# Four modulation channels as row products on TensorE in the mixer's front, in place of dot products on VectorE

## The chip, the cores and the metric

The kernel runs on one core of a Trainium2 chip. A core has TensorE (PE in the profile; its weight loads are PEld), VectorE (DVE), ScalarE (ACT), GpSimd (POOL), and SyncE (SP), whose queue issues the DMA transfers here. The metric is the device time of one launch in microseconds (us), lower is better.

## What is computed

One layer of a diffusion backbone on 1024 latent tokens and 256 context tokens of width 1024: a SwiGLU block, a mixer (gated linear attention beside a gated spatial MLP), a second SwiGLU block, a final norm. The layer is modulated by nine channels of 1024 numbers, computed from a condition vector:

```python
def adaln(cond, w, b):
    return (jax.nn.silu(cond) @ w + b).reshape(cond.shape[0], ADA_MODS, 1, D_MODEL)
...
x = x + 0.5 * m_x[:, 2] * swiglu(modulate(rmsnorm(x, g1), m_x[:, 0], m_x[:, 1]), ff1_in, ff1_out)
y_x = modulate(rmsnorm(x, g2), m_x[:, 3], m_x[:, 4])
...  # mixer on y_x and on the context's y_c
x = x + m_x[:, 5] * mix_x
x = x + 0.5 * m_x[:, 8] * swiglu(modulate(rmsnorm(x, g3), m_x[:, 6], m_x[:, 7]), ff2_in, ff2_out)
```

So channel 5 is first needed by the mixer's output projection, channels 6 and 7 by the norm in front of the second block, and channel 8 by that block's last sums. `w` is 1024 x 9216 in fp32, 4 MB per channel. Channels 0 to 4 are needed for the latent condition `c` and for the context's `c_ctx`, channels 5 to 8 for `c` alone.

## The kernel before

Everything lies with the model's width on the 128 partitions, in 8 tiles (`NK`), and tokens along the free dimension, in blocks of 512, 512 and 256 (`TBS`). Matmuls that need accuracy are split into a high and a low part and run as three products (`gemm`, L357 to L360). The two SwiGLU blocks (`ffn`) are written as a seven-product scheme over pairs of 512-token blocks (`winograd`, L492).

The program is written in an order that a planner then changes: at build time it simulates all engines and takes, for each engine, the ready instruction that was written earliest (code in `high_priority` goes ahead). The order on each engine's queue is fixed then, and on the chip each engine works its queue in that order. Tiles come from pools by tag, with a fixed number of buffers per tag (`BUFS`): `raw` (2) takes weights as they land from DRAM, `w` (6) their high and low parts, `ar` (2) takes small loads and the dot products' weights, `po`, `pg` and `pn` are banks of PSUM, the accumulators (3, 3 and 2).

Modulation is done in two ways. Channels 0 and 1 (`ada_first`, `ada_rows`, `ada_cols`) are row products on PE at the very start: the condition's tile, 128 x 2, is the stationary operand, a weight tile of 128 x 1024 streams past it in two halves (L206), and after eight tiles a row of 2 x 1024 lies in PSUM; ScalarE copies it out, and small matmuls against the identity turn it into columns (L216). Channels 2 to 8 (`ada_part`) are dot products on VectorE: the weights are stored transposed (`wb`), a tile of 128 x 512 lands in `ar` (L167), and one instruction (L169, output `junk`, not used) multiplies it with the condition, which lies as a row on all partitions (`cr`, `cond_row`), and sums along the free dimension. There are 16 such tiles to a channel; after the last, L175 adds the halves and L155 the bias. Channels 2 to 4 are done during the first block, channels 5 to 7 in the mixer (48 tiles, written after the attention's second half), and channel 8 during the second block (16 tiles, `ada_todo`).

The mixer (`mixer`) begins with `mixer_front`: eight tiles of q, k and v are projected (`qkv_gemm`, output `z`), convolved by VectorE (`conv`, L791) and, for v, transposed (`tr`, L841). Each takes its weights through `raw` (L132), ScalarE makes the high part (L142), GpSimd the low one (L143). Then come the attention's states, scores and outputs (`ds` L1055, `sc` L1110, `o`). The gating's projections (`fill`: `vs`, `ogu`) are written late, and the planner puts them into PE's gaps from the front on. Next are the spatial gating (`gmlp_mix`, `mx`) and the output projection (`wo_add`): 32 sums of 12 matmuls each (`wo`), and each is added to x on VectorE with channel 5 as the scale (L1372). After each half of the tokens, `done2` computes the norm and the operands of the second block (`right_ops`, L453, L444), with channels 6 and 7.

Of the kernel before, what the change touches and what calls it, by code (L numbers as in the profile page):

```python
# [11 lines left out]
AF = mybir.ActivationFunctionType  # L12
ALU = mybir.AluOpType
# [3 lines left out]
P = 128  # L17
NK = 8
# [8 lines left out]
class Layer:  # L27
# [150 lines left out]
    def cond_row(self, j, c, dst):  # L178

        nc = self.nc  # L180
        n = c.stop - c.start
        t = self.tile(self.sb, 512, "ar", "cv")[:, :n] if n <= 512 else dst
        nc.sync.dma_start(t, self.a["cvec"][j:j + 1, c].to_broadcast([P, n]))
        nc.scalar.activation(dst, t, AF.Silu)
# [35 lines left out]
    def ada_first(self):  # L220

        pr = [[self.po("row") for _ in range(2)], [self.pg("row") for _ in range(2)]]
        for i in range(NK):
            for ch in range(2):
                self.ada_rows(self.a["wa"][ch], pr[ch], i)
        for ch in (1, 0):
            self.ada_cols(ch, pr[ch])

    def norm_coef(self, chs, gcol, nj, s):
# [733 lines left out]
    def mixer_front(self, y):  # L963

        nc, a = self.nc, self.a
# [29 lines left out]
        for dt in range(2):  # L995
            self.qkv_conv(ko[dt], 2 + dt, [self.k[0, dt], self.k[1, dt]], self.k[2, dt])
        vc = self.m("vc")
        for h in range(4):
            ct = self.h("ct")
            t = self.qkv_tile(y, a["wi"][2 + h], 4 + h, None, ct[:, :256])  # L1000
            if h % 2 == 0:
                v = [self.d("v") for _ in range(2)]
# [317 lines left out]
    def mixer(self, y, done=None):  # L1320
        nc, a = self.nc, self.a
# [6 lines left out]
        q1 = [self.queries(1, dt) for dt in range(2)]  # L1328
        row = self.d("cr")
        self.cond_row(0, slice(0, 1024), row)  # L1330
        for ch in (5, 6, 7):
            for h in range(2):
                for dt in range(NK):
                    self.ada_part(ch, dt, h, [row[:, h * 512:h * 512 + 512]])
        self.fill(y)
# [41 lines left out]
    def run(self):  # L1377
        nc, a = self.nc, self.a
# [67 lines left out]
        def done2b(tb):  # L1446
# [3 lines left out]
            for k in range(NK):  # L1450
# [5 lines left out]
                else:  # L1456
# [5 lines left out]
        self.ffn(mov, None, a["ff2i"], a["ff2o"], gates2, load_x2, None, self.squares(accs),  # L1462
                 done2b, self.ada_todo((8,), 1, 1, 16))

# [16 lines left out]
def pack(i):  # L1481
# [11 lines left out]
    o = {}  # L1493
# [14 lines left out]
    wa = i["w_ada"][0]  # L1508
    o["wa"] = c(wa.reshape(NK, P, 9, 1024)[:, :, :2].transpose(2, 0, 1, 3))
    o["wb"] = c(wa[:, 2048:].T.reshape(7, 8, P, 1024))  # L1510
    for s in ("ff1", "ff2"):
# [32 lines left out]
```

## Time and profile before

| | us |
|---|---|
| median of 3 runs | 2159.13 (2155.48 to 2160.04) |
| the profiled execution's own time | 2155.53 |
| its span, first to last instruction | 2153.8 |
| PE busy | 2015.6 |
| VectorE busy | 1503.2 |
| ScalarE busy | 816.5 |
| GpSimd busy | 379.9 |

Times inside the trace count from the span's start. The first block lies from about 120 to 900 us, the mixer from 930 to 1450, the second block behind it. A matmul's busy time is modelled and matmuls overlap in the pipeline, so the distance from one start to the next tells what a matmul costs, and a busy share near 100% tells that PE has no gaps. In fp32 a matmul shows as two records.

### The profile page before, as it was taken

Reading aid. Unit: us, or ns where it says so; the run is one execution under the profiler, and the core shown is the slowest. Engines: PE = TensorE matmul, PEld = TensorE weight load, DVE = VectorE, ACT = ScalarE, POOL = GpSimd, SP = SyncE. Lnnn points to the kernel's source line nnn. Section 1 sums busy time; section 2 is a strip of 40 time slices with the busy share of each in tenths; the row PEclk is TensorE's granted clock in tenths of the full one; section 3 lists DMA queues with packets and bytes.
Section 4 is the critical chain, followed back from the end, with each engine's and each line's share of the span. In section 5 each row is a group of like instructions: output and inputs, shape, how many; then the busy total and the mean of one; then the engine's idle time right before and its main releaser. Section 6 shows DMA issues by size and latency. Waiting matters only on the chain.

```text
span 2153.8 us, 28445 instructions
## 1 busy us (share of the span) xinstructions
PE 2015.6 (94%) x10868; PEld 1669.6 (78%) x10868; DVE 1503.2 (70%) x2503; ACT 816.5 (38%) x1297; POOL 379.9 (18%) x215
## 2 busy tenths in 40 slices
PE   6799999999999999898999998787999999999997
PEld 1678888888887888787788877565888888868875
DVE  3976665656655779869888377778677786755585
ACT  3643333333333121256456345325343444442111
POOL 0000000000025555223210010300000000065740
PEclk9799999999999999999999899897999999999998
DMA  7033333333368786321111126550444343458742
GB/s 286 25 127 118 123 142 118 122 118 118 118 222 340 275 295 240 147 79 54 49 56 50 35 91 219 200 183 28 166 158 165 112 181 137 182 216 350 306 143 79
DMA packets 111273, 332.27 MB, mean 154 GB/s; under 512 B 12448, under 2 KB 15392, under 8 KB 111136
## 3 DMA queue, kind: packets, MB, share of 16 engines
q1 hardware_dynamic: 111136, 330.45, 41.8%
q8 instruction: 85, 1.39, 0.3%
q14 instruction: 52, 0.43, 0.1%
HBM read 231.31 MB, written 99.09 MB: 153 GB/s over the span
## 4 chain that ended last, share of the span: by engine, by line
PE 72%; DVE 18%; DMA 5%; issue 2%; ACT 2%; POOL 0%; SPq 0%; DVEq 0%; ACTq 0%
PE c L492 14%; PE a L492 14%; PE f L492 14%; PE b L492 7%; DVE acc L791 3%; DMA ar<-in_wb 2%; PE gc L541 2%; PE gc L540 2%; PE gc L539 2%; PE row L206 1%; DVE hl L444 1%; PE o L541 1%; PE o L539 1%; PE o L540 1%; DVE junk L169 1%
## 5 line engine op out<-in xcount | busy, mean ns | idle before, releaser
L384 POOL TENSOR_TENSOR s<-raw 128x512 f32<-128x512 f32 x18 | 23.8, 1322 | 1149.0 <-DVE ch L526 602.0
L169 DVE SCALAR_TENSOR_TENSOR junk<-ar,cr 128x512 bf16<-128x512 f32 x160 | 112.5, 703 | 58.6 <-DMA ar<-in_wb 44.1
L390 ACT ACTIVATE gh<-raw 128x1024 fp32r<-128x1024 f32 x62 | 65.7, 1059 | 171.6 <-PE c L492 64.1
L492 PE MATMUL f<-hl,uh 128*128 128x512 f32 x528 | 126.8, 389 | 0.0
L443 ACT ACTIVATE hl<-g 128x512 fp32r<-128x512 f32 x106 | 64.3, 626 | 157.4 <-DVE g L526 153.0
L492 PE MATMUL a<-hl,gh 128*128 128x512 f32 x352 | 114.4, 403 | 8.8 <-ACT hl L443 6.3
L492 PE MATMUL c<-hl,sh 128*128 128x512 f32 x352 | 111.1, 393 | 11.7 <-ACT hl L443 9.6
L394 ACT ACTIVATE sh<-s 128x1024 fp32r<-128x1024 f32 x62 | 65.5, 1057 | 147.1 <-PE a L492 87.1
L492 PEld LDWEIGHTS f<-hl,uh 128*128 128x128 f32 x528 | 99.1, 188 | 20.6
L492 PE MATMUL b<-hl,gh 128*128 128x512 f32 x352 | 112.3, 396 | 0.8 <-ACT hl L443 0.8
L492 PE MATMUL a<-hl,sh 128*128 128x512 f32 x352 | 110.1, 393 | 1.0 <-ACT g L567 1.0
L492 PE MATMUL f<-hl,th 128*128 128x512 f32 x352 | 110.2, 390 | 0.8 <-ACT hl L443 0.8
L492 PE MATMUL c<-hl,th 128*128 128x512 f32 x352 | 108.9, 391 | 0.0
L526 DVE TENSOR_TENSOR u<-c,u 128x512 f32<-128x512 f32 x44 | 30.2, 687 | 109.0 <-ACT u L577 109.0
L791 DVE SCALAR_TENSOR_TENSOR acc<-z,par,acc 128x945 f32<-128x945 f32 (+2 forms) x64 | 93.1, 1477 | 11.6 <-ACT acc L813 10.5
L143 POOL TENSOR_TENSOR wl<-raw,wh 128x1024 fp32r<-128x1024 f32 x20 | 52.0, 2606 | 257.5 <-ACT wh L142 257.2
L444 DVE TENSOR_TENSOR hl<-g,hl 128x512 fp32r<-128x512 f32 x106 | 74.9, 724 | 26.1 <-ACT hl L443 26.0
L492 PEld LDWEIGHTS c<-hl,sh 128*128 128x128 f32 x352 | 66.4, 189 | 27.4 <-ACT hl L443 10.2
L385 DVE TENSOR_TENSOR sl<-s,sh 128x1024 fp32r<-128x1024 f32 x44 | 54.8, 1246 | 45.2 <-PE gc L540 21.9
L492 PEld LDWEIGHTS a<-hl,gh 128*128 128x128 f32 x352 | 67.1, 195 | 23.0 <-ACT hl L443 6.8
L492 PEld LDWEIGHTS b<-hl,gh 128*128 128x128 f32 x352 | 67.3, 191 | 15.8 <-ACT hl L443 1.8
L492 PEld LDWEIGHTS a<-hl,sh 128*128 128x128 f32 x352 | 66.6, 189 | 15.7 <-ACT g L567 1.3
(342 smaller groups left out, 6030.6 us busy)
## 6 DMA issues: line engine op xcount, KB each, us to landing
hd<-hl SPq DMA_DIRECT2D x142, 512.0 KB, 3.6
hc<-hd SPq DMA_DIRECT2D x142, 512.0 KB, 7.4
ar<-in_wb SPq DMA_DIRECT2D x112, 256.0 KB, 3.1
raw<-in_ff1i SPq DMA_DIRECT2D x44, 512.0 KB, 3.7
raw<-in_ff2i SPq DMA_DIRECT2D x44, 512.0 KB, 4.5
raw<-in_ff1o SPq DMA_DIRECT2D x22, 512.0 KB, 4.9
raw<-in_ff2o SPq DMA_DIRECT2D x22, 512.0 KB, 4.8
x<-in_xT SPq DMA_DIRECT2D x16, 512.0 KB, 6.8
```

The lines of the kernel that those rows point to most:

```text
L143: eng.tensor_tensor(out=lo[:, :n], in0=src[:, :n], in1=hi[:, :n].bitcast(F32), op=ALU.subtract)
L169: i = nc.vector.scalar_tensor_tensor(out=self.junk, in0=w, scalar=1.0, in1=cbc[j], op0=ALU.mult, op1=ALU.mult, accum_out=acc[:, h, dt, j:j ...
L385: sub = lambda o, x, y: eng.tensor_tensor(out=o, in0=x, in1=y, op=ALU.subtract)
L390: nc.scalar.activation(gh, g, AF.Copy)
L394: nc.scalar.activation(sh, s, AF.Copy)
L443: nc.scalar.activation(t[:, :512], src, AF.Copy)
L444: nc.vector.tensor_tensor(out=t[:, 512:], in0=src, in1=t[:, :512].bitcast(F32), op=ALU.subtract)
L492: mm = lambda x, y, start, stop: nc.tensor.matmul(ps, x, y, start=start, stop=stop, skip_group_check=more)
L539: nc.tensor.matmul(ps, hi[:, c], mh, start=i == 0, stop=False)
L540: nc.tensor.matmul(ps, hi[:, c], ml, start=False, stop=False)
L541: nc.tensor.matmul(ps, lo[:, c], mh, start=False, stop=i == n - 1)
L791: self.nc.vector.scalar_tensor_tensor(out=o, in0=zv[:, r0 + dr:r1 + dr, c0 + dc:c1 + dc], scalar=self.par[:, tap:tap + 1], in1=o, op0=ALU. ...
```

## The change

`ada_steps` is new: a generator that computes channels as row products on PE. For each pair of weight tiles it loads both through `raw` and issues four matmuls, each into its own group of 32 columns of PE's array (`g` = 0, 32, 64, 96: two weight tiles by two halves of 512). After eight tiles the four partial rows, two partitions each, are copied by ScalarE into a tile that was zeroed by VectorE, and a matmul with a selecting matrix `sel` adds the two groups of a half and turns them into columns. In `mixer_front`, channels 5, 6, 7 and 8 are made so, four steps behind each of v's four projections, one channel to a projection. The dot products of channels 5 to 7 in `mixer` and of channel 8 in the second block go, with their rows of the condition. The weights of these channels are stored as rows (`wa`) and no longer transposed (`wb`).

```diff
--- before.py
+++ after.py
@@ -179,7 +179,7 @@
 
         nc = self.nc
         n = c.stop - c.start
-        t = self.tile(self.sb, 512, "ar", "cv")[:, :n] if n <= 512 else dst
+        t = self.tile(self.sb, 512, "ar", "cv")[:, :n]
         nc.sync.dma_start(t, self.a["cvec"][j:j + 1, c].to_broadcast([P, n]))
         nc.scalar.activation(dst, t, AF.Silu)
 
@@ -225,6 +225,34 @@
                 self.ada_rows(self.a["wa"][ch], pr[ch], i)
         for ch in (1, 0):
             self.ada_cols(ch, pr[ch])
+
+    def ada_steps(self, chs):
+
+        nc = self.nc
+        sel = self.const([P, 2, 2], "sel")
+        for h in range(2):
+            nc.vector.tensor_tensor(out=sel[:, h], in0=self.ident[:, 32 * h:32 * h + 2],
+                                    in1=self.ident[:, 64 + 32 * h:66 + 32 * h], op=ALU.add)
+        for i, ch in chs:
+            pr = self.pn("row")
+            for k in range(0, NK, 2):
+                wts = [self.load(self.a["wa"][i, k + e]) for e in range(2)]
+                for e in range(2):
+                    for h in range(2):
+                        g = 64 * e + 32 * h
+                        nc.tensor.matmul(pr[g:g + 2], self.sc[:, k + e, :], wts[e][:, h * 512:h * 512 + 512],
+                                         start=(k == 0), stop=(k == NK - 2))
+                if k == NK - 2:
+                    row = self.h("row")
+                    nc.vector.memset(row, 0.0)
+                    for g in range(0, P, 32):
+                        nc.scalar.activation(row[g:g + 2], pr[g:g + 2], AF.Copy)
+                    pt = self.po("cols")
+                    for dt in range(NK):
+                        nc.tensor.matmul(pt[:, 2 * dt:2 * dt + 2], row[:, dt % 4 * P:dt % 4 * P + P], sel[:, dt // 4],
+                                         start=True, stop=True)
+                    self.ada_bias(ch, 2, pt[:, :2 * NK].rearrange("p (k j) -> p k j", j=2))
+                yield
 
     def norm_coef(self, chs, gcol, nj, s):
         A = self.const([P, NK, 2], "A" + s)
@@ -995,9 +1023,12 @@
         for dt in range(2):
             self.qkv_conv(ko[dt], 2 + dt, [self.k[0, dt], self.k[1, dt]], self.k[2, dt])
         vc = self.m("vc")
+        ada = self.ada_steps([(2, 5), (3, 6), (4, 7), (5, 8)])
         for h in range(4):
             ct = self.h("ct")
             t = self.qkv_tile(y, a["wi"][2 + h], 4 + h, None, ct[:, :256])
+            for _ in range(4):
+                next(ada)
             if h % 2 == 0:
                 v = [self.d("v") for _ in range(2)]
             for tb in range(2):
@@ -1326,12 +1357,6 @@
         on = [self.gla_norm(0, g0, [self.queries(0, dt) for dt in range(2)])]
         g1 = self.gla(1)
         q1 = [self.queries(1, dt) for dt in range(2)]
-        row = self.d("cr")
-        self.cond_row(0, slice(0, 1024), row)
-        for ch in (5, 6, 7):
-            for h in range(2):
-                for dt in range(NK):
-                    self.ada_part(ch, dt, h, [row[:, h * 512:h * 512 + 512]])
         self.fill(y)
         gm = self.gmlp_norm()
         with self.tc.high_priority():
@@ -1460,7 +1485,7 @@
 
         accs = {}
         self.ffn(mov, None, a["ff2i"], a["ff2o"], gates2, load_x2, None, self.squares(accs),
-                 done2b, self.ada_todo((8,), 1, 1, 16))
+                 done2b)
 
 
 def out_units(w):
@@ -1506,8 +1531,8 @@
         m[:, l] = ((np.arange(P)[:, None] % 64) >> l) ^ (np.arange(64)[None, :] >> l) == 1
     o["masks"] = m.reshape(P, 6 * 64)
     wa = i["w_ada"][0]
-    o["wa"] = c(wa.reshape(NK, P, 9, 1024)[:, :, :2].transpose(2, 0, 1, 3))
-    o["wb"] = c(wa[:, 2048:].T.reshape(7, 8, P, 1024))
+    o["wa"] = c(wa.reshape(NK, P, 9, 1024)[:, :, [0, 1, 5, 6, 7, 8]].transpose(2, 0, 1, 3))
+    o["wb"] = c(wa[:, 2048:5120].T.reshape(3, 8, P, 1024))
     for s in ("ff1", "ff2"):
         o[s + "i"] = c(col_tiles(i[s + "_in"][0]).reshape(2, NF, P, 1024).transpose(1, 0, 2, 3))
         o[s + "o"] = out_units(i[s + "_out"][0])
```

## Rows read from the trace of the kernel before

**Rows 1.** The page's totals: busy us, share of the span, instructions.
```profile
PE 2015.6 (94%) x10868; PEld 1669.6 (78%) x10868; DVE 1503.2 (70%) x2503; ACT 816.5 (38%) x1297; POOL 379.9 (18%) x215
```
**Rows 2.** The page's chain that ended last, shares of the span by line.
```profile
PE c L492 14%; PE a L492 14%; PE f L492 14%; PE b L492 7%; DVE acc L791 3%; DMA ar<-in_wb 2%; PE gc L541 2%; PE gc L540 2%; PE gc L539 2%; PE row L206 1%; DVE hl L444 1%; PE o L541 1%; PE o L539 1%; PE o L540 1%; DVE junk L169 1%
```
**Rows 3.** Busy us (and instructions) per stretch; then PE clock, DMA share, GB/s.
```profile
core 0: us, PE busy (x) PEld busy (x) DVE busy (x) ACT busy (x) POOL busy (x), PEclk, DMA share, GB/s
...
990.00:1050.00 60.00, 51.69 (x266) 43.07 (x265) 48.50 (x57) 37.08 (x71) 13.54 (x5) 0.97 0.19 62
1050.00:1115.00 65.00, 64.44 (x406) 57.79 (x405) 60.87 (x63) 27.73 (x52) 11.40 (x4) 1.00 0.13 43
1115.00:1180.00 65.00, 60.59 (x854) 54.39 (x853) 54.27 (x99) 41.81 (x76) 9.43 (x4) 0.97 0.18 60
...
1240.00:1320.00 80.00, 77.40 (x732) 62.42 (x730) 53.49 (x101) 46.70 (x77) 11.56 (x7) 0.94 0.40 139
1320.00:1344.00 24.00, 19.79 (x167) 15.41 (x166) 22.42 (x55) 5.62 (x9) 1.29 (x1) 1.00 0.57 195
1344.00:1356.00 12.00, 0.91 (x2) 0.81 (x3) 5.43 (x13) 5.41 (x6) 0.00 (x0) 0.59 0.96 375
1356.00:1450.00 94.00, 85.29 (x355) 65.86 (x354) 72.56 (x146) 22.80 (x36) 16.20 (x9) 0.98 0.53 173
1450.00:1503.00 53.00, 34.22 (x116) 24.86 (x116) 48.72 (x88) 33.69 (x56) 0.00 (x0) 0.77 0.12 41
```
**Rows 4.** PE's waits, 1320 to 1450: us in total, times, longest us.
```profile
PE wo L357 <- DVE x L1372: 19.5, 13, 11.6
```
**Rows 5.** VectorE's timeline: start us, us, instruction, idle time before it and its releaser.
```profile
1351.10 0.69 DVE L169 SCALAR_TENSOR_TENSOR junk<-ar,cr 128x512 bf16<-128x512 f32 x1 [5.15 <-DMA ar<-in_wb]
...
1353.61 0.17 DVE L155 TENSOR_TENSOR mods<-acc,par 128x8 f32<-128x8 f32 x1
...
1428.19 0.16 DVE L155 TENSOR_TENSOR mods<-acc,par 128x8 f32<-128x8 f32 x1
```
**Rows 6.** Groups by line, 1290 to 1450: busy us, mean ns, idle before, releasers.
```profile
L169 DVE SCALAR_TENSOR_TENSOR junk<-ar,cr 128x512 bf16<-128x512 f32 x48 | 36.4, 759 | 43.8 <-DMA ar<-in_wb 30.0 <-ACT cr L184 13.6
```
**Rows 7.** Tile wo, third of its three lines: min, median, max ns; first and last start.
```profile
L360 PE MATMUL wo<-ah,wo x128: 388/389/628, 1325.1 to 1449.0; 128*128 128x512 f32 x128
```
**Rows 8.** The chain in order of time: start us, us, what, instructions merged.
```profile
16.34 25.84 PE row L206 x60
42.18 2.78 PE cols L216 x24
...
123.17 2.72 PE c L492 x12
...
1165.31 1.02 PE ds L1055 x16
...
1172.04 0.44 PE tr L841 x4
...
1193.30 2.77 PE ds L1055 x48
...
1340.64 9.12 DMA og<-ogu
```
**Rows 9.** Busy us in a stretch of the second block, columns as in rows 3.
```profile
1920.00:1940.00 20.00, 18.23 (x75) 13.21 (x74) 6.64 (x12) 6.86 (x11) 13.32 (x8) 1.00 1.01 408
```
**Rows 10.** PE's timeline in the attention's scores.
```profile
1125.94 1.10 PE L1110 MATMUL sc<-x 64*64 64x64 f32 x60
```
**Rows 11.** DMA issues, 930 to 1130: KB each, median us to landing.
```profile
raw<-in_wi SPq DMA_DIRECT2D x10, 512.0 KB, 3.5
```
**Rows 12.** Groups by line, 990 to 1112, columns as in rows 6.
```profile
L143 POOL TENSOR_TENSOR wl<-raw,wh 128x1024 fp32r<-128x1024 f32 x9 | 24.9, 2771 | 89.4 <-ACT wh L142 89.4
...
L142 ACT ACTIVATE wh<-raw 128x1024 fp32r<-128x1024 f32 x9 | 9.6, 1072 | 17.7 <-issue 7.2 <-PE z L359 6.3 <-PE ogu L359 4.2
```
**Rows 13.** SP's timeline: the issue behind the first buffer given out.
```profile
984.67 0.33 SPq L132 DMA_DIRECT2D raw<-in_wi  x1
```
**Rows 14.** Tile z, 985 to 1100: min, median, max ns; first and last start.
```profile
L360 PE MATMUL z<-y,wl x144: 277/389/632, 995.0 to 1094.2; 128*128 128x512 f32 x96, 128*128 128x256 f32 x48
```

## The prediction, made before the change was run

> **What bounds the kernel now.** I read the engine totals first [rows 1]: TensorE (PE) is busy 94% of the span and VectorE (DVE) 70%, so a microsecond of PE work is dear and a microsecond of DVE work is cheap unless a stage says otherwise. Next the chain of waits as a whole [rows 2]: matmul lines lead it, but 2% is the landing of `ar<-in_wb`, the transposed weights of the dot products that the change removes, and 1% their instruction (`junk`, L169). So the removed work stands on the path somewhere, with about 43 + 20 us. Then the mixer by stages [rows 3], where the reader is to see two different regimes. From 990 to 1320 us PE is full: 51.7 of 60, 64.4 of 65, 60.6 of 65 and, at the end, 77.4 of 80 us. From 1344 to 1450 it is not: 0.9 of 12, then 85.3 of 94, and 34.2 of 53 us behind that. The change puts work into the first regime and takes work out of the second.
>
> Why PE stands still from 1343 to 1355 is in the waits and VectorE's timeline [rows 4, 5]: the output projection waits 19.5 us in all for the addition at L1372, once 11.6 us, because that addition multiplies by channel 5, whose last dot product (1351.10) had waited 5.15 us for its weights; the bias row (L155) follows at 1353.61, the additions behind it. For channels 6 and 7 it comes as late as 1428.19. In between VectorE works its queue in order, dot products and additions mixed. Over all it waits 30.0 us for weights, and 13.6 us before that for the row of the condition [rows 6]. PE has three accumulators for the projection, so each such wait soon reaches it.
>
> **The removed part, mixer.** The 48 dot products take 36.4 us of VectorE and 43.8 us of idle time before them [rows 6]. Not all of this is the kernel's: the time is what PE loses. The projection has 3 x 128 matmuls from 1325.1 to 1449.0 [rows 7]; at 12 in 2.72 us [rows 8] that is 87 of 124 us. Less some 7 us of other matmuls in between (the last of the gating, the spread of a norm), 30 us are lost, 11.6 of them for channel 5. The last reload, og, lands at 1349.8 [rows 8] and is needed only for the projection's second half, so PE would run on from about 1344; some 5 us of matmuls of the second block's first tiles also lie in that gap. I count 23 us gained to the end of the projection. After it, 1450 to 1503 is VectorE's (48.7 of 53 us busy [rows 3]): the norm and the operands of the second block for both halves of the sequence. The first half (8 modulations and 8 splits, 16 x 0.7 us, about 11 us) could run beside the second half of the projection, but waited for channels 6 and 7 and for the same queue. I count 8 of the 11. In 1320 to 1344 VectorE is busy 22.4 of 24 us with a dozen dot products (8 us) between the gating's additions; worth perhaps 1 us to PE. Sum 32 us; the bounds are 20 (the projection finds its next wait at the reloads of x and og) and 42 (30 + 11 + 1).
>
> **The removed part, second block.** 16 dot products of channel 8, 11 us of VectorE, and 4.2 MB of loads. PE is busy 18.2 of 20 us in 1920 to 1940, with the DMA engines full (1.01) [rows 9]. At 408 GB/s each 256 KB load is 0.64 us, 10 us for the sixteen if all fell in full stretches; PE shows 1.8 us lost in this one. I take 2 us (0 to 4).
>
> **The added part, PE.** Four channels x 8 weight tiles x 2 halves = 64 matmuls, 128 rows x 2 columns by 512, each two records. The nearest rows are the same matmuls at the start of the kernel, one after the other: 60 records in 25.84 us, 0.431 us each [rows 8]. In one column group the 128 records would be 55 us. The four groups may run side by side. Two groups of 64 columns do: 48 records `ds` in 2.77 us, 0.058 us each, where four full-width records `tr` of the same 128 elements take 0.44, 0.110 each, so 1.9 times as fast [rows 8]. Four tiles of 64 x 64 give 60 records in 1.10 us with ends included, 0.018 us each [rows 10], against half of 0.110 alone: three times. Four column groups at full height are not in the trace. Bounds: 55 / 4 = 14 us and 55 / 2 = 28 us (a pair of matmuls from one weight tile together, the other weight tile not there yet); below nothing cannot be, as all of it is new. I take 22. The Trainium skill, "TensorE: Matmul & The Clock Gate", section "Part 3: Packing small matmuls", says that matmuls start and end in strict order without reordering: as the two records of one matmul share a group, that rule would allow only pairs, 28 us in place of 22, and the whole sum would be -5, inside the range that I give the forecast. The trace speaks against it as a general limit, since in [rows 10] more than two records run at once.
>
> Entering and leaving the tiled shape costs about 0.1 us (16 `ds` records alone among others take 1.02 us, a third of 48 takes 0.92 [rows 8]); 16 to 32 times: 3 us. Turning the rows into columns: per channel 8 matmuls, 16 records, at 24 in 2.78 us [rows 8], 7.4 us for four. Sum on PE: 22 + 3 + 7.4 = 32 us (24 to 38). From 990 to 1050 PE idles 8.3 us and from 1115 to 1180 another 4 [rows 3], about 9 of which the new work can fill. All later PE work in the mixer (the projections kept in reserve for its gaps) is only pushed back, since PE is full to 1320. Net 23 us later.
>
> **The added part, everything else.** 16 copies on ScalarE of some 0.6 us (half of the 1024-wide copy's 1.07 [rows 12], rounded up), 10 us: hidden, ScalarE is busy 37 of 60 and 28 of 65 us there [rows 3]; uncovered they would hold 0.6 us of the cols matmuls each time. Four memsets and small sums on VectorE, 3 us: VectorE is busy 60.9 of 65 us there, but its queue waits for PE's tiles, so a later PE hides them. 32 loads of 512 KB by SP: the DMA share there is 0.13 to 0.19, 16.8 MB fit. But they go through `raw`, which has two buffers, ahead of the weights of the next projection tile in program order. One load holds its buffer for the landing (median 3.5 us [rows 11]), a pair of matmuls (0.9) and a wait for PE's order (about 0.9): 5.3 us, 2.65 per load with two buffers. A projection tile holds one for 3.5 us, ScalarE's 1.07 and GpSimd's 2.77 [rows 12]: 7.3, or 3.7. From 984.7 us, when a buffer is next given out [rows 13]: 32 x 2.65 + 5 x 3.7 = 103 us, so q's last weights come at about 1088, its matmuls (2 x 24 x 0.227 = 11 us per tile) end near 1108 instead of 1094.2 [rows 14]. That is 14 us, less than PE's 23: by this account the buffers don't set the end. Behind a waiting load on SP stand the stores of projected tiles, whose three buffers ScalarE needs; there are few in this stretch.
>
> **Sum.** +23 - 32 - 2 = -11 us against the profiled execution's 2155.53 us (span 2153.8): 2144.5. That execution lies 3.6 us under the median of the runs shown, 2159.13, so on that footing 2148.
>
> **Rivals.**
> 1. *Both buffers of `raw` become the bound: slower.* For it: SP already waits on them, matmuls and loads alternate on two buffers, and PE can do nothing else without weights that come through the same two. Against it: the account above leaves 9 us. It decides once a load holds its buffer for over 5.9 us ((23 - 14) / 32 x 2 more than 5.3), and makes the kernel slower from 6.6 us on (34 us late). At 7.5 us, one more wait of 2 us: 32 x 3.75 + 18 = 138 us from 985, q ends near 1143, 49 us late: +49 - 32 - 2 = +15, 2174.
> 2. *Full packing.* Groups run four at a time, the pairs arrive together, and the steps fall into gaps: PE 24, minus 10 of gaps, 14 net: 14 - 36 - 2 = -24, 2135. For it: [rows 10]. Against it: weight tiles land one by one.
> 3. *The gain goes elsewhere.* Projection and VectorE find the next wait (x and og reloads, then VectorE's 49 us for the second block): gain 20 only: +23 - 20 - 2 = +1, 2160. For it: og takes 9.1 us to land [rows 8], and VectorE is full from 1450 on. Against it: the dot products' own loads, 12.6 MB, leave that stretch.
> 4. *The steps don't pack at all:* 55 + 10 us, net 56: 56 - 34 = +22, 2181. The rows of two groups speak against it; I fold it into the first.
>
> **How the numbers follow.** Chances: forecast 0.47 (own range 2138 to 2158), rival 1 with 4 0.26, rival 2 0.17, rival 3 0.10. The best ends together, 14 - 42 - 4 = -32, give 2127, with 4 us below them for a plan made anew; above, rival 1's price is the end, and what is worse (49 - 20 = +29 and rival 4) is left out as about a tenth: 2123 to 2173. About 0.2%, 4.3 us, is what a measurement can tell from no change. Faster: 0.9 of the forecast's cases and rival 2, 0.59; slower: 0.26; the rest, most of rival 3, 0.15.
>
> **What would show it.** Right: no wait of L1372 near 1343, the projection's 384 matmuls in under 100 us, the second block's first full stretch some 10 us shorter behind it; the end of the q tiles' matmuls 15 to 30 us later than 1094; records of the new matmuls overlapping, two to four in 0.43 us. Wrong: PE idle in the front for loads of `in_wa`, new matmuls 0.43 us apart, or the projection still waiting as long. The schedule is planned anew for the whole mixer, so a different order of the reserve work could move either term by some 5 us.

## The result, and the profile after

The changed kernel took 2229.89 us (median of 4 runs, 2229.08 to 2231.8) against 2157.31 us (2152.95 to 2160.04) of the kernel before on the same chip: ratio 1.034 [1.0319, 1.036], 72.6 us slower. The forecast was 2148, the range 2123 to 2173.

The gain behind the front came as forecast. The front did not cost 23 us, but about 100.

Tiles z and wo of the changed kernel, third of their three lines, against [rows 14] and [rows 7]; lines L360, L357 and L1372 of before are L388, L385 and L1397 here:

```profile
L388 PE MATMUL z<-y,wl x144: 277/389/542, 1000.0 to 1193.5; 128*128 128x512 f32 x96, 128*128 128x256 f32 x48
...
L388 PE MATMUL wo<-ah,wo x128: 387/389/499, 1432.3 to 1527.4; 128*128 128x512 f32 x128
```

The last `z` matmul of the front starts at 1193.5 in place of 1094.2, 99.3 us later. The output projection starts 107.2 us later (1432.3 against 1325.1; of the 7.9 us more, 6.0 are one wait for ScalarE in the scan that grew from 0.7 to 6.7 us), takes 95.1 us in place of 123.9 (28.8 gained) and ends 78.4 us later. The span is 2230.0 against 2153.8, 76.2 longer, so another 2.2 us come back behind it, nearly all before the second block's first `c` matmul, which is at 1554.3 against 1478.2, 76.1 later. Sum: +107.2 - 28.8 - 2.2 = +76.2 us.

The wait of [rows 4] in the changed kernel (us in total, times, longest us):

```profile
PE wo L385 <- DVE x L1397: 1.2, 1, 1.2
```

19.5 us became 1.2. In the chain of waits by line, `junk` (L169) is no longer listed, and `ar<-in_wb` is now the weights of channels 2 to 4 in the first block alone; the loads of the rows' weights have come in (`DMA raw<-in_wa`), and the front's lines L385, L387 and L243, which [rows 2] does not have:

```profile
PE c L520 13%; PE f L520 13%; PE a L520 13%; PE b L520 7%; DMA ar<-in_wb 3%; DMA raw<-in_wa 2%; DVE acc L554 2%; PE gc L569 2%; PE gc L568 2%; PE gc L567 2%; PE row L206 1%; PE z L385 1%; DVE hl L472 1%; PE z L387 1%; PE row L243 1%
```

By stretches, to be read against [rows 3]:

```profile
core 0: us, PE busy (x) PEld busy (x) DVE busy (x) ACT busy (x) POOL busy (x), PEclk, DMA share, GB/s
990.00:1050.00 60.00, 49.46 (x233) 33.92 (x234) 42.17 (x59) 32.15 (x63) 5.57 (x2) 0.80 0.30 102
1050.00:1115.00 65.00, 48.78 (x218) 30.06 (x214) 21.51 (x23) 14.02 (x26) 2.35 (x1) 0.79 0.35 107
1115.00:1180.00 65.00, 49.90 (x204) 31.96 (x205) 13.16 (x15) 18.59 (x31) 9.41 (x4) 0.74 0.40 128
```

The regime in which PE was full is gone: 48.8 of 65 us where 64.4 were, and the granted clock, 0.97 to 1.00 before, is 0.74 to 0.80, a mixture of 1.2 and 2.4 GHz. No other engine is busy in its place, and the DMA share is 0.30 to 0.40. So nothing is at its limit; things wait for each other. PE's only waits from 1015 to 1170, and the longest wait of SP's queue from 1015 to 1180 (us in total, times, longest us):

```profile
PE row L243 <- DMA raw<-in_wa: 31.9, 15, 3.7
PE cols L252 <- ACT row L249: 9.9, 4, 2.5
...
SPq L132 <- PE row L243: 104.1, 28, 16.7
```

PE waits for the rows' weights and for ScalarE's copies of the rows, and SP waits for PE to be done with a buffer. How this comes about is in the timeline of one channel (start us, us, instruction, idle time before it and its releaser), first PE and ScalarE, then SP's issues:

```profile
1020.20 1.04 PE L243 MATMUL row<-raw,sc 128*2 128x512 f32 x8
...
1024.91 1.03 PE L243 MATMUL row<-raw,sc 128*2 128x512 f32 x4 [3.67 <-DMA raw<-in_wa]
...
1026.22 1.71 PE L243 MATMUL row<-raw,sc 128*2 128x512 f32 x4 [0.28 <-DMA raw<-in_wa]
...
1029.60 1.87 PE L243 MATMUL row<-raw,sc 128*2 128x512 f32 x4 [1.67 <-DMA raw<-in_wa]
...
1037.65 1.88 PE L243 MATMUL row<-raw,sc 128*2 128x512 f32 x4 [0.69 <-DMA raw<-in_wa]
...
1039.57 2.39 ACT L249 ACTIVATE row<-row 2x512 f32<-2x512 f32 x4 [4.04 <-PE row L243]
...
1041.98 1.06 ACT L142 ACTIVATE wh<-raw 128x1024 fp32r<-128x1024 f32 x1
...
1042.01 3.57 PE L252 MATMUL cols<-sel,row 128*128 128x2 f32 x16 [2.48 <-ACT row L249]
...
1045.44 1.95 PE L869 MATMUL tr<-ident,acc 128*128 128x128 f32 x8
...
1047.04 0.78 PE L385 MATMUL z<-y,wh 128*128 128x512 f32 x1
...
1063.90 1.04 PE L243 MATMUL row<-raw,sc 128*2 128x512 f32 x8
```

```profile
988.25 0.33 SPq L132 DMA_DIRECT2D raw<-in_wa  x1
...
1021.27 13.29 SPq L132 DMA_DIRECT2D raw<-in_wa  x6
...
1037.00 0.33 SPq L132 DMA_DIRECT2D raw<-in_wi  x1
...
1045.49 0.33 SPq L132 DMA_DIRECT2D raw<-in_wa  x1
...
1050.94 0.33 SPq L132 DMA_DIRECT2D raw<-in_wa  x1
...
1064.97 0.80 SPq L132 DMA_DIRECT2D raw<-in_wa  x2
```

The reader is to see three things that follow one another. The first load, issued at 988.25, waits in its buffer for PE's turn at 1020.20. From there to 1037.00 PE only takes row products as further loads land one by one (16.8 us; six in all, the sixth at 1037.65, with waits of 0.3 to 3.7 us). Then SP gets a buffer for the next projection tile (`in_wi`, 1037.00), and PE's first matmul with it is at 1047.04, 10.0 us later. In this time PE ends the channel: the last row step (1037.65), the wait for ScalarE's four copies (2.48 us), the columns to 1045.58, a few transposes. ScalarE splits the tile's high part behind its copies, by 1043.04, so here it is not the tile that PE waits for; by the list above PE never does. Then PE streams that tile to 1063.90 (16.9 us, a row step at 1049.45 among it), and meanwhile the two loads issued at 1045.49 and 1050.94 sit in both buffers, until SP issues again at 1064.97. That is 43.7 us for a value tile and a channel; the mean from channel to channel is 41.1 us (the sums of channels 5 and 8 come at 1045.6 and 1168.8).

### The profile page after: what moved, and what is told of

It reads as the page before. It is cut to its first block, busy times and chain, and to the rows that moved or that the text cites. A ratio compares the mean times of both kernels' runs of the same rounds, so it can differ in the third digit from the quotient of the medians.

```text
span 2230.0 us, 28613 instructions
## 1 busy us (share of the span) xinstructions
PE 2078.3 (93%) x11060; PEld 1697.3 (76%) x11060; DVE 1446.8 (65%) x2377; ACT 825.0 (37%) x1309; POOL 384.5 (17%) x215
## 4 chain that ended last, share of the span: by engine, by line
PE 74%; DVE 14%; DMA 7%; ACT 2%; issue 2%; SPq 0%; POOL 0%; DVEq 0%; ACTq 0%
PE c L520 13%; PE f L520 13%; PE a L520 13%; PE b L520 7%; DMA ar<-in_wb 3%; DMA raw<-in_wa 2%; DVE acc L554 2%; PE gc L569 2%; PE gc L568 2%; PE gc L567 2%; PE row L206 1%; PE z L385 1%; DVE hl L472 1%; PE z L387 1%; PE row L243 1%
## 5 line engine op out<-in xcount | busy, mean ns | idle before, releaser
L819 DVE SCALAR_TENSOR_TENSOR acc<-z,par,acc 128x945 f32<-128x945 f32 (+2 forms) x64 | 82.8, 1307 | 65.8 <-ACT acc L841 64.9
L418 ACT ACTIVATE gh<-raw 128x1024 fp32r<-128x1024 f32 x62 | 65.6, 1059 | 159.2 <-PE c L520 48.8
L554 DVE TENSOR_TENSOR u<-c,u 128x512 f32<-128x512 f32 x44 | 30.2, 686 | 109.6 <-ACT u L605 109.6
L520 PEld LDWEIGHTS c<-hl,sh 128*128 128x128 f32 x352 | 66.5, 189 | 27.3 <-ACT hl L471 10.2
L169 DVE SCALAR_TENSOR_TENSOR junk<-ar,cr 128x512 bf16<-128x512 f32 x96 | 65.3, 680 | 22.2 <-DMA ar<-in_wb 21.2
```

What stands on the lines that cost most here:

```text
L169: i = nc.vector.scalar_tensor_tensor(out=self.junk, in0=w, scalar=1.0, in1=cbc[j], op0=ALU.mult, op1=ALU.mult, accum_out=acc[:, h, dt, j:j ...
L418: nc.scalar.activation(gh, g, AF.Copy)
L520: mm = lambda x, y, start, stop: nc.tensor.matmul(ps, x, y, start=start, stop=stop, skip_group_check=more)
L554: tt = lambda eng, o, x, y, op: eng.tensor_tensor(out=o, in0=x, in1=y, op=op)
L819: self.nc.vector.scalar_tensor_tensor(out=o, in0=zv[:, r0 + dr:r1 + dr, c0 + dc:c1 + dc], scalar=self.par[:, tap:tap + 1], in1=o, op0=ALU. ...
```

## The experiments

Theory A: the two `raw` buffers and PE's order pass the new loads and the projections' weights one behind the other. Theory B: PE's own new work (its packing, its clock) is the cost. Theory C: ScalarE's row copies, which stand ahead of the next split. Each run's difference is to the kernel before on the same chip; "period" is the mean distance of the channels' sums.

| run | median us | difference us | ratio, 95% interval | last z us | period us |
|---|---|---|---|---|---|
| changed kernel | 2229.9 | +72.6 | 1.034 [1.0319, 1.036] | 1193.5 | 41.1 |
| x1_none | 2124.2 | -36.1 | 0.9833 [0.9801, 0.9865] | 1094.9 | - |
| x2_resident | 2145.2 | -15.1 | 0.9922 [0.9899, 0.9944] | 1115.8 | 19.0 |
| x3_loads | 2198.2 | +37.9 | 1.0176 [1.0143, 1.0209] | 1162.0 | 34.0 |
| x4_open | 2194.6 | +34.2 | 1.0159 [1.0127, 1.019] | 1165.0 | 34.1 |
| x5_ar | 2255.0 | +94.2 | 1.0436 [1.04, 1.0471] | 1153.9 | 57.6 |
| x6_ar_open | 2254.7 | +93.9 | 1.0434 [1.04, 1.0468] | 1148.0 | 58.1 |
| x7_fill | 2237.3 | +76.5 | 1.0353 [1.0327, 1.0378] | 1094.0 | 36.3 |
| y1_crh | 2156.6 | -4.2 | 0.9979 [0.9967, 0.9991] | 1093.3 | - |
| x8_w | 2155.5 | -1.0 | 0.9989 [0.9978, 1.0001] | 1126.0 | 27.3 |
| x8_w_open | 2159.9 | +3.3 | 1.0003 [0.9986, 1.002] | 1130.5 | 27.7 |
| z1 (5 to 7) | 2151.3 | -5.2 | 0.9977 [0.9961, 0.9993] | 1116.0 | 27.5 |
| z2 (5) | 2147.9 | -11.6 | 0.995 [0.9934, 0.9966] | 1100.7 | - |
| z3 (5, 6) | 2147.4 | -12.2 | 0.9949 [0.9929, 0.9968] | 1110.2 | 30.4 |

**x1_none: the gain alone.** The steps' loads and matmuls are gone; the bias alone is added.

```diff
-                wts = [self.load(self.a["wa"][i, k + e]) for e in range(2)]
...
-                    self.ada_bias(ch, 2, pt[:, :2 * NK].rearrange("p (k j) -> p k j", j=2))
+                    self.nc.vector.tensor_copy(
+                        self.mods[:, ch],
+                        self.par[:, C_BADA + 8 * ch:C_BADA + 8 * ch + 8].unsqueeze(2).to_broadcast([P, NK, 2]))
```

> The changed kernel without any row product: channels 5 to 8 hold their bias alone (their products with the condition are left out of the computation). The tail's gain stays, the front's cost goes. Theory A (the two `raw` buffers pass the new loads and the projections' weights one behind the other) and theory B (the new matmuls' own time on PE, slow clock and order) say the same: the last z and q matmul at 1094 to 1100 us as before (1193.5 in the changed kernel), the projection's 384 matmuls in some 97 us as in the changed kernel, total 2157 - 31 = 2126 us (2115 to 2135). If the total stays above 2150, the tail's gain was not there and both fall.

36.1 us faster by the medians, 30.2 by the profiled spans (2123.6 against 2153.8; the profiled execution of before, 2155.53, lies 5 us under 2160.33, the median of the kernel before on this run's chip). The front is that of before (last z 1094.9), the projection takes 95.6 us. So the gain is there in full, and the row products cost the changed kernel 108.7 us (+72.6 against -36.1), 98.6 of them by the last z matmul.

**x2_resident: PE's work without loads.**

```diff
+        res = self.h("res")
+        nc.sync.dma_start(res, self.a["wa"][2, 0, :, :512])
...
-                wts = [self.load(self.a["wa"][i, k + e]) for e in range(2)]
...
-                        nc.tensor.matmul(pr[g:g + 2], self.sc[:, k + e, :], wts[e][:, h * 512:h * 512 + 512],
+                        nc.tensor.matmul(pr[g:g + 2], self.sc[:, k + e, :], res,
```

> All 64 row matmuls stay, with their shape and place, but stream one 128x512 weight tile that is loaded once into another buffer; the 32 loads through `raw` are gone (the true weights of channels 5 to 8 are left out). Theory A (buffers): the front costs only PE's work, 24 to 38 us: last z matmul at about 1120 (1112 to 1130), total 2145 to 2165. Theory B (PE's own time): the last z matmul stays near 1180 to 1195, total 2215 to 2232. Theory C (ScalarE's four row copies per channel stand ahead of the next tile's split, 2.4 us times 4 channels): would leave at most 10 us above theory A's figure.

21.0 us above x1_none, and the last z 20.9 us later: all that PE's own work and the copies cost without loads. Theory B falls as the main cause, and C with it, since the copies on ScalarE are all still there; behind late rows they cost PE the 9.9 us of waits shown above. The timeline, the group of the row products (busy us, mean ns, idle before), and the first stretch:

```profile
1031.34 3.62 PE L244 MATMUL row<-res,sc 128*2 128x512 f32 x32
1040.86 1.84 PE L253 MATMUL cols<-sel,row 128*128 128x2 f32 x16
...
L244 PE MATMUL row<-res,sc 128*2 128x512 f32 x128 | 15.3, 592 | 0.0
...
990.00:1050.00 60.00, 55.40 (x332) 42.46 (x331) 48.49 (x59) 38.42 (x73) 12.70 (x5) 0.97 0.16 49
```

32 records in 3.62 us is 0.113 each, a fourth of the 0.431 of [rows 8]: where the weights are there, four column groups run side by side.

**x3_loads: the loads with little of PE's work.** Each row matmul streams 2 columns, and ScalarE copies 2 in place of 512.

```diff
-                        nc.tensor.matmul(pr[g:g + 2], self.sc[:, k + e, :], wts[e][:, h * 512:h * 512 + 512],
+                        nc.tensor.matmul(pr[g:g + 2, :2], self.sc[:, k + e, :], wts[e][:, h * 512:h * 512 + 2],
...
-                        nc.scalar.activation(row[g:g + 2], pr[g:g + 2], AF.Copy)
+                        nc.scalar.activation(row[g:g + 2, :2], pr[g:g + 2, :2], AF.Copy)
```

> All 32 loads of 512 KB through `raw` stay, in their place, but each row matmul streams 2 columns in place of 512 (the rest of channels 5 to 8 is left out). PE's new work is almost nothing. Theory A (buffers): a load still holds its buffer until its matmul, so only about 0.9 us of some 8.8 us per pair goes: the last z matmul at 1165 to 1190, total 2195 to 2228. Theory B (PE's own time): last z matmul near 1100 to 1110, total 2126 to 2140.

74.0 us above x1_none, as theory A has it; the total is inside what was expected, the last z, 1162.0, 3 us before it. Of PE's new work the columns' matmuls are left (14.3 us busy) and 5.6 us of rows. PE's waits for loads, 1015 to 1140 us:

```profile
PE row L243 <- DMA raw<-in_wa: 46.3, 21, 3.7
```

Loads 74, matmuls 21, both 108.7: at least 14 us, since the columns' matmuls are in both runs, are where the one makes the other longer.

**x4_open: the projection's weights first.** The same steps, but the next projection tile is loaded and split ahead of the channel's steps.

```diff
-            t = self.qkv_tile(y, a["wi"][2 + h], 4 + h, None, ct[:, :256])
+            for tb in range(3):
+                self.qkv_gemm(o, y, 4 + h, tb, ct[:, :256])
+            nxt = self.qkv_open(a["wi"][3 + h])
+            t = self.qkv_conv(o, 4 + h, None, ct[:, :256])
+            o = nxt
```

> The whole computation; the weights of the next projection tile are loaded and split before the channel's four steps in place of behind them, so that PE has a full projection tile to stream while the eight loads of a channel pass the two `raw` buffers. Theory A (order in the buffers): eight loads at 2.65 to 3.7 us each are 21 to 30 us, beside them 14 us of a projection tile plus 8 of new work: a period of 25 to 32 us in place of 41, the last z matmul 35 to 65 us earlier (1130 to 1160), total 2165 to 2195. If the order is all that costs, 2150. Theory B (PE's own time): no change, 2222 to 2232.

The total is at the upper edge of what theory A expected; the period of 34.1 us misses its 25 to 32, and the last z, 1165.0, its 1130 to 1160. The order in the buffers is worth 38 us (72.6 - 34.2), a third of the 108.7 us. Nine loads in 34.1 us are 3.8 us each, so a buffer is held 7.6 us, though the loads land as fast as before (in_wa, issues from 1015 to 1160: KB each, median us):

```profile
raw<-in_wa SPq DMA_DIRECT2D x30, 512.0 KB, 3.7
```

The other 3.9 us would then be the matmuls and the wait for their turn in PE's order, which now stands among the projection's matmuls; this is worked out, not seen.

**x5_ar and x6_ar_open: own buffers, half tiles.** The rows' weights come as 128x512 halves through the two buffers `ar`; x6_ar_open has x4_open's order as well.

```diff
-                wts = [self.load(self.a["wa"][i, k + e]) for e in range(2)]
...
+                        wt = self.tile(self.sb, 512, "ar", "wa")
+                        nc.sync.dma_start(wt, self.a["wa"][i, k + e, :, h * 512:h * 512 + 512])
```

> The whole computation; the row products' weights come as 128x512 halves (256 KB) through the two buffers `ar` and no longer through `raw`, which keeps only the projections' weights. Order and place unchanged. Theory A as the runs so far sharpen it (PE's part is 21 us, the rest of the front's cost is that loads and projection weights pass two buffers in turn): the projection tiles can be fetched while a channel's loads run, so the two chains lie beside each other: 16 halves by some 4 us through two buffers are 32 us per channel if a half lands as slowly as a whole tile, 24 if it lands in 3: a period of 24 to 33 us in place of 41, total 2165 to 2200. Theory A' (the shared buffers are the whole cost, a half lands fast): 2145 to 2155. Theory B (PE's own time and slow clock): 2225 to 2232.

> x5_ar and x4_open together: own buffers, and the next projection tile's weights opened before the channel's four steps. If what x4_open left (34 us per channel) was that the eight loads and the projection's load still share two buffers, own buffers give a shorter period here, 22 to 30 us, and a total of 2150 to 2185, below both x4_open and x5_ar. If it was the time that two buffers take to pass 4.2 MB at one load of 3.6 us each, whichever buffers they are, it stays within 10 us of the better of the two.

Both miss far, upwards; x6_ar_open also misses its 10 us around the better of the two, which was x4_open. For x5_ar a load of a half and the row products' group:

```profile
wa<-in_wa SPq DMA_DIRECT2D x64, 256.0 KB, 2.7
```

```profile
1175.24 1.02 PE L244 MATMUL row<-wa,sc 128*2 128x512 f32 x2
...
L244 PE MATMUL row<-wa,sc 128*2 128x512 f32 x128 | 65.0, 599 | 11.9 <-DMA wa<-in_wa 11.9
```

Half the bytes land in 2.7 us where the whole tile takes 3.6 to 3.7, so two buffers of halves bring less per us. The Trainium skill, "SBUF — State Buffer", section "The DMA setup-cost knee (why "@ 1 MiB" ≠ asymptote)", says that each transfer pays some 2 us whatever its size; the 2.7 us for half the bytes agree with that direction. And with one half there at a time one column group runs alone: the row products take 65.0 us of PE in place of 15.3. That is the case of rival 4, made by the landing and not by TensorE. It is not the whole of the 94 us. PE waits only 11.9 us for these loads. The scan comes behind the last row step: its first scores start at 1258.3 (1203.0 in the changed kernel). The reserve of projections is used up among the row steps (PE 100.0 of 100 us busy from 1155 to 1255), and from 1258 to the output projection the granted clock is 0.75, with 15.1 us of waits for VectorE (L1126; 0.2 at the same line of the changed kernel). So these two runs say little on the buffers alone.

**x7_fill: the same steps in the reserve of projections.**

```diff
+        ada = self.ada_steps([(2, 5), (3, 6), (4, 7), (5, 8)])
         for j in (6, 7, 0, 1, 2, 3):
...
                 self.project(w, y, j, tb, self.last_level if j == 3 and tb else None)
+                for _ in range(2):
+                    next(ada, None)
```

> The whole computation; the sixteen steps move from the front's value tiles to the reserve of projections (`fill`), two behind each projected half, where `raw` gives out a buffer only some ten times between 1100 and 1320 us in the kernel before. Theory A: the loads then land beside the scan's matmuls, only PE's 21 us stay, and the tail keeps its gain of 36: the last z matmul at 1094 to 1100, total 2140 to 2160, as with the resident weight tile (2145). If instead the scan's order leaves PE waiting for single loads there too, 2160 to 2190. Theory B: above 2200.

A miss: the front is free of it (last z 1094.0), but the same cost appears in the scan. The total lies where theory B was put, above 2200; it is x2_resident and x8_w that speak against B, not this run. From 1230 to 1390 us:

```profile
L243 PE MATMUL row<-raw,sc 128*2 128x512 f32 x128 | 43.2, 773 | 24.4 <-DMA raw<-in_wa 24.1
```

The steps were planned back to back, 1234.6 to 1373.0, and again two loads at a time feed them. The granted clock is 0.70 to 0.79 there. Buffers that stand idle on average don't help steps that come in a bunch.

**x8_w: six buffers.** Whole tiles again, loaded into `w`.

```diff
-                wts = [self.load(self.a["wa"][i, k + e]) for e in range(2)]
+                wts = [self.w("wa") for _ in range(2)]
+                for e in range(2):
+                    nc.sync.dma_start(wts[e], self.a["wa"][i, k + e])
```

> The whole computation; the 512 KB tiles of the row products are loaded into buffers of the tag `w` (six, of which a projection tile needs two) in place of `raw`, so that up to four of them can be under way at once and `raw` is left to the projections' weights. Whole tiles, so a pair of records in two column groups comes with each landing, as in the changed kernel. Theory A'' (what costs is the number of loads under way: a buffer's hold, landing plus the wait for PE's order, divided by the buffers): eight holds of 5 to 8 us over four buffers are 10 to 16 us per channel, beside them 14 us of projection and 5 of new work on PE: a period of 19 to 25 us, last z and row matmul near 1120 to 1140, total 2145 to 2170. If landing time is a matter of bytes and not of buffers (256 KB halves through `ar` came at 1.87 us each), the pace stays 3 us per tile and more: total 2195 to 2230. Theory B (PE's own time, slow clock): 2225.

> As x8_w, and the next projection tile's weights are opened (loaded and split) before the channel's four steps, so two of the six `w` buffers stand ready and fewer are left to the new loads. If the number of loads under way is what counts, no better than x8_w and up to 20 us worse; if the late projection weights still cost, 5 to 20 us better than x8_w.

This settles it between the buffers and PE's own work. The same loads, matmuls and copies, written at the same place, take 2155.5 us in place of 2229.9, by another tag for a buffer. The tag changes two things at once: there are six buffers, and the rows' weights no longer share `raw` with the projections' (in `w` they stand beside these tiles' high and low parts). Total and last z are within what was expected, the period of 27.3 us above its 19 to 25. The timeline of the first channel, the group of the row products, and the stretches:

```profile
1017.34 1.90 PE L245 MATMUL row<-wa,sc 128*2 128x512 f32 x16
1021.01 1.03 PE L245 MATMUL row<-wa,sc 128*2 128x512 f32 x4 [1.77 <-DMA wa<-in_wa]
1022.42 1.03 PE L245 MATMUL row<-wa,sc 128*2 128x512 f32 x4 [0.39 <-DMA wa<-in_wa]
...
L245 PE MATMUL row<-wa,sc 128*2 128x512 f32 x128 | 24.0, 592 | 7.3 <-DMA wa<-in_wa 7.3
```

```profile
990.00:1050.00 60.00, 54.81 (x315) 41.01 (x315) 47.73 (x62) 36.29 (x71) 8.32 (x3) 1.00 0.45 161
1050.00:1115.00 65.00, 62.34 (x326) 40.84 (x323) 34.38 (x31) 27.14 (x47) 11.59 (x5) 1.00 0.51 176
```

Four tiles stand ready for the first channel, 16 records run in 1.90 us, and the clock stays at 1.00. Row products take 24.0 us of PE and wait 7.3; in the changed kernel it was this group:

```profile
L243 PE MATMUL row<-raw,sc 128*2 128x512 f32 x128 | 41.7, 838 | 31.9 <-DMA raw<-in_wa 31.9
```

Opening the projections early on top of it (x8_w_open) brings nothing, as was expected if the number of loads under way counts.

**y1_crh: the gain without the move.** The kernel before, its dot products started earlier by another buffer for the condition's row.

```diff
-        row = self.d("cr")
-        self.cond_row(0, slice(0, 1024), row)
+        rows = [self.h("cr") for _ in range(2)]
+        for h in range(2):
+            self.cond_row(0, slice(h * 512, h * 512 + 512), rows[h])
```

> The kernel before, dot products on VectorE and all, but the condition's row stands in two 512-wide `h` buffers in place of a 1024-wide `d` buffer, which came free only at 1292 us: the dot products may start in VectorE's idle time between 1180 and 1240 us, and channel 5 is done before the projection needs it. If what the change gained behind the front (31 to 36 us) was the late start of the dot products, this gains much of it with nothing on PE: 2125 to 2145. If it was VectorE's share of work itself, 2150 to 2160. If the dot products delay the scan's own additions, slower than 2160.

4.2 us: the gain of an early start (2125 to 2145) is missed, and the total lies in the 2150 to 2160 put for VectorE's share of work itself. Channel 5 is done at 1293.0 in place of 1353.6 and the projection takes 105.1 us in place of 123.9, but it starts 19.7 us later. The dot products now stand among the scan's additions, and PE's waits in the scan have grown, for L1094 from 0.8 us (1166 to 1330) to 4.7 (1166 to 1342), in all from 2.8 to 11.7; the granted clock from 1220 on is 0.76 to 0.80, 0.88 to 0.89 in the kernel before.

```profile
L360 PE MATMUL wo<-ah,wo x128: 387/389/628, 1344.8 to 1449.9; 128*128 128x512 f32 x128
```

```profile
PE sc L1110 <- DVE x L1094: 4.7, 2, 3.5
```

The early start alone is not the gain; by this run VectorE's work has to go, though the planner also ordered the scan anew.

**z1, z2, z3: how many channels pay.** As x8_w with three channels, one or two as rows; the others stay dot products as before. z2:

```diff
-        ada = self.ada_steps([(2, 5), (3, 6), (4, 7), (5, 8)])
+        ada = self.ada_steps([(2, 5)])
...
+        row = self.d("cr")
+        self.cond_row(0, slice(0, 1024), row)
+        for ch in (6, 7):
...
-                 done2b)
+                 done2b, self.ada_todo((8,), 1, 1, 16))
```

> As x8_w, but channel 8 stays with VectorE's dot products in the second block, as in the kernel before: three channels of rows in the front. The second block gained nothing measurable from the move of channel 8 (0 to 1 us in the changed kernel and in the one without row products), while each channel costs PE about 5 us in the front plus its share of waits. Theory A'': 5 to 10 us below x8_w, total 2138 to 2162. If channel 8's loads do cost the second block 2 us or more, 2 to 7 below x8_w.

> Only channel 5 as rows in the front, its weights through the six `w` buffers; channels 6 to 8 stay VectorE's dot products at their old places. If cost and gain go by channel: the front costs 6 to 9 us (a fourth of the 31 by which the last z matmul came later with all four through `w`), the projection no longer waits 11.6 us for channel 5 and VectorE has 16 dot products fewer (12 us) ahead of its additions: gain 12 to 20, total 2157 - 4 to - 13 = 2144 to 2153. If the wait for channel 5 is only handed on to the next late operand (the reloads, channels 6 and 7 at 1400 to 1428 us), gain below 8 and no difference from the kernel before within 0.2%.

> As z2 with channels 5 and 6 as rows. If cost and gain go by channel: the front costs 13 to 16 us, the gain is between that of one and that of three channels: total 2142 to 2153, between z2 and z1. If the second block's first operands wait for channel 7 alone, no better than z2.

All three totals lie in what was expected; that z3 would lie between z2 and z1 did not show, as z2 and z3 are the same. z1 lies 4.2 us under x8_w, not the 5 to 10 of theory A'': that is in the 2 to 7 put for a second block which does gain by channel 8's move. Tile wo of z2, z3 and z1:

```profile
L390 PE MATMUL wo<-ah,wo x128: 388/390/398, 1337.5 to 1440.1; 128*128 128x512 f32 x128
```

```profile
L390 PE MATMUL wo<-ah,wo x128: 388/390/402, 1342.0 to 1439.7; 128*128 128x512 f32 x128
```

```profile
L390 PE MATMUL wo<-ah,wo x128: 388/389/502, 1349.7 to 1439.9; 128*128 128x512 f32 x128
```

Against 1325.1 to 1449.0 [rows 7], channel 5 shortens the projection by 21.3 us and delays its start by 12.4. Channel 6 shortens it by 4.9 more and delays it by 4.5, channel 7 by 7.5 and 7.7: they pay for themselves and no more. z2 and z3 are 0.5% faster than the kernel before, and so faster than the changed one too.

## Why the prediction was wrong

**The step that failed** is the account of the buffers under "The added part, everything else": "a wait for PE's order (about 0.9): 5.3 us, 2.65 per load with two buffers", and from it "by this account the buffers don't set the end". The pace inside a burst was as priced: the six issues from 1021.27 on end 13.29 us later, five steps of 2.6 us and the last issue itself. But 0.9 us is the wait when PE has nothing else. The two loads at each tile's boundary wait for a whole projection tile: the buffers given out at 1045.49 and 1050.94 are given out again from 1064.97 on, holds of 19.5 and about 14 us. And the account added ring time (24.9 us per channel) beside PE time (14 of a value tile, 48 matmuls at 0.227 and 24 at 0.12 us, and 8 of new work), as if both ran at once. The projection's weights pass the same two buffers, in program order behind the channel's last load, so PE has nothing to stream while the row loads come one by one, and only two loads can come while it streams. The two take turns: 16.8 us of row steps, 10.0 for the channel's end, 16.9 of projection in the channel shown, 41.1 in the mean. From the trace of before one could have read it: a value tile takes PE 14 us, a buffer's hold was put at 5.3, and only two loads fit beside it.

**Rival 1** named the mechanism, the place and the sign; its price, one more wait of 2 us on each hold (+15 us), was too low, and so was the worst end named, +29, against +72.6. x3_loads and x8_w show the mechanism; the size of 74 us is x3_loads' alone.

**PE's added work: the net right, in part by luck.** 23 us net forecast, 20.9 measured (x2_resident). Within it the rows and their change of shape were taken at 25 us and the rows take 15.3, which is rival 2's full packing; the cols were taken at 7.4 and take 4 x 1.84 = 7.4. Of the 9 us of gaps that were to swallow part of it little came: 22.7 us of work made the front 20.9 later, and PE's idle time from 990 to 1050 fell only from 8.3 to 4.6 us. The two misses cancel. In the changed kernel the same rows take 41.7 us and the columns 14.3, since tiles come singly, and at a lower clock: four records of one tile take 1.88 us behind a wait (granted clock 0.50 from 1029.0 to 1039.6), 1.03 in x8_w. The Trainium skill's strict order ("TensorE: Matmul & The Clock Gate", section "Part 3: Packing small matmuls — row/col tiling") would, as the prediction read it, have allowed pairs, 28 us; the 15.3 us go against that reading.

**ScalarE's copies.** They were taken as hidden, or at 0.6 us each time uncovered. They are hidden in x2_resident and x8_w; behind late rows PE waits for all four, 2.5 us a channel.

**The mixer's tail: right in sum.** 32 forecast. The changed kernel has 28.8 in the projection (23 forecast) and most of 2.2 behind it (8 forecast); x1_none 30.2 over the whole span. About 6 us more of it lies in the projection than I put there, and 6 less behind it; that these cancel is luck.

**The second block: open.** 2 us forecast. From its first `c` matmul to the end of the span it is 675.7 us against 675.6 before: nothing. But z1, z2 and z3, which leave channel 8 to VectorE, take 678.6 to 679.4 there, and x8_w 674.7. With one trace of each, a gain of 0 to some 4 us is what can be said.

**What the forecast would have been worth with the buffers right:** x2_resident, with PE's part and the gain, took 2145.2, the forecast being 2148. By the differences to the kernel before of their own batches, the steps above x1_none (-36.1) are: PE's work 21 (-15.1); weights through six buffers 14 more (-1.0); through two that they share with the projections, these opened first, 35 more (+34.2); with the projections behind them, 38 more (+72.6).

**Open.** How much of the last two steps, 35 and 38 us, is the lower clock and how much the waits themselves was not separated: no kernel here has the waits at the full clock. In the changed kernel PE's own waits in the front are 41.8 us (31.9 + 9.9) of the 108.7. Nor was the number of buffers separated from the sharing: no run has more `raw` buffers, or two whole ones of the rows' own. Nor is it shown why channel 8 as a row makes the projection of x8_w longer again (97.1 us against z1's 90.2); the order of the whole mixer is planned anew in each.

## What to carry to other kernels

Before moving streamed work onto a busy engine, follow one buffer of the ring through one whole period, with the longest thing that can stand ahead of its consumer in the engine's order, not the typical one; if another stream uses the same ring, price the two in turn unless there are buffers enough for both. Test the parts apart: the matmuls with a resident tile, and the loads with matmuls cut to almost nothing, cost two runs and give both prices. And move one channel before moving four: here the first one carries the whole net gain.

## What the runs showed of the hardware

Four column groups of 128 rows by 2 columns run together when issued together: 32 records in 3.62 us (x2_resident), 16 in 1.90 (x8_w), 8 in 1.04 (changed kernel), ends included, and 4 (two groups) also in 1.03 (x8_w). A group alone costs PE as much: 2 records in 1.02 us (x5_ar). So a landing that brings one half tile at a time undoes the packing entirely. A load of 256 KB took 2.7 us and one of 512 KB 3.6 to 4.1 with two buffers (changed kernel, x4_open, x3_loads); with more under way in x8_w the median rose to 4.7 us, while the stretch moved 161 to 176 GB/s in place of 102 to 107.
